# 512-column products with v, row-by-row reads of the second merge branch, and a later place in the queue for the pairs of the last product, in an encoder layer on Trainium2

## The chip, the cores and the metric

The kernel is one program on one core of a Trainium2 chip. The metric is device time in microseconds (us). The kernel before took 1592.64 us in the median of three runs (1591.06 to 1593.86). Rates and waits below come from one profiled execution of it, read with the hardware profiler.

## The reference

The reference is one layer of an encoder with three branches, for two sequences of 512 rows and 1024 columns each. Cut to what matters here:

```python
h = rmsnorm(x) @ w_in
u, q, k, v, xq, g = split(h)                      # g: three gates of 1024 columns
y_s5 = s5_branch(u)                               # state-space scan, both directions
w = softmax(q0 @ k0.T) - lam * softmax(q1 @ k1.T) # 4 heads, two maps each
y_diff = rmsnorm(w @ v) * (1 - lambda_init)       # 4 heads of 128 columns
y_x = cross_attention(xq, mem)
merged = sum(sigmoid(g[n]) * (branch[n] @ w_up[n]) for n in range(3))
x = x + merged @ w_out
gate, up = split(rmsnorm(x) @ w_ffn_in)           # 2816 columns each
x = x + (silu(gate) * up) @ w_ffn_out
out = rmsnorm(x)
```

All data is float32, and the result has to have nearly float32 precision.

## The kernel before, in words

**Precision.** TensorE multiplies in a reduced float32 format (fp32r). Each operand is therefore split into a high and a low part: ScalarE (ACT) rounds the source to the high part and VectorE (DVE) subtracts it for the low part (`split`, lines 134 to 138). One product is then three matmuls: high by high, high by low, low by high. A matmul has 128x128 weights and streams 512 columns, or 256 in the products with v. Every matmul and every transpose is issued through one helper (lines 66 and 69), so in the profile they all have one of these two lines, and they are told apart by the tiles in their names. Nearly all of the order of TensorE's work from the attention on is the order in the code (`InOrder`).

**Attention.** For each of 4 heads and 2 sequences there are 4 steps of 128 query rows (`qt` 0 to 3). A step i of the loop near line 915 does: scores for two steps at once (every other step), ten further matmuls or so from a queue of other work (`fill`), then `turn(i)`, then `outputs(i - 1)` after every second step, then more filling. `turn` transposes the 128x512 weights of the softmax on TensorE into a bank named `tr` (seen as `bktr`), and splits them into `pH` and `pL`; a pair of these tiles holds two steps, 256 columns, and there are four buffers, two pairs. `outputs` multiplies one such pair by v: 12 matmuls of 256 columns (tiles `bkoo<-pH,vh` and so on). It runs twice per head and sequence, in two halves of one bank, and ScalarE copies the bank to `osb` after the second (line 892). `squares` and `normed` (line 911) then normalise `osb` and write it to DRAM (`bD`).

**Merge.** Other work in that queue is `merges`: for each of 8 column tiles m, first branch 0, then branch 2, later branch 1. `merge_units` reads a gate row `gl` (1024 columns, 512 KB) into the ring `ld`, which has four slots, and multiplies the products by it on VectorE (line 796). The branches themselves are read as rows `yt` into the same four slots and split into `yh`, `yl` (line 773 the read, lines 137 and 138 the split). Branch 2's four rows are read and split together ahead of tile m = 2 of branch 0.

**Feed-forward.** 22 iterations, 19 us each, make seven products of a Strassen-like scheme (`SEVEN`) for each 128 rows of hidden units. GpSimd (POOL) makes sums of the weights (`ws`, lines 1040 to 1043) and multiplies `up` (line 1182). From iteration 4 on, a `half_piece` per iteration also prepares raw weights of the last product: sums on POOL (lines 454 to 457), splits, and a write to DRAM (`wD`). It is held behind two instructions of the iteration, the tanh and the last sum. The activations `ac` are written to DRAM tiles `aD[0..21]`.

**Last product.** `VISITS` lists 12 visits v of an output tile, 36 pieces in all, each a pair p of hidden tiles. A piece is 21 matmuls: seven products, three matmuls each. It needs three things: its prepared weights `w` (pieces 0 to 15 come whole from `wD`, two reads of 384 and 512 KB, lines 1255 and 1253; pieces 16 to 27 half; pieces 28 to 35 are prepared on the spot from raw weights), the pair's activations, and room. A pair is two reads of 512 KB (`fa` and `fb`, lines 1139 and 1140), four sums on VectorE and POOL (lines 989 to 992) and four splits into `th` and `tl`. Pairs 3 to 8 are brought in by `pair_in` at set places of the loop. After visits, VectorE and POOL add the seven banks into `y` (lines 1120 and 1308).

**Who issues reads.** Nearly all DMAs are issued by SyncE (SP), which takes its list in order and waits where a buffer is not free yet. The list is built by a scheduler; `queued()` means that what is issued inside it stands behind the last weight read issued so far (`last_w`). `tc.issue_after(x)` holds instructions behind x in their engines' lists.

## Time and profile before

| | |
|---|---|
| median of three runs | 1592.64 us (1591.06 to 1593.86) |
| the profiled execution | 1595.11 us |
| its span in the trace | 1593.3 us, so 1.8 us lie around the span |
| TensorE busy | 99% of the span, 7838 matmuls and transposes |
| VectorE, ScalarE, GpSimd busy | 73%, 40%, 33% |
| mean granted TensorE clock | 0.996 |
| DMA | 237.84 MB, 149 GB/s in the mean |

The granted clock is given as a share of full speed. Matmuls are pipelined: a matmul of 512 columns is shown 0.39 us long, but the next one starts about 0.23 us after it. How long a stretch of matmuls takes is therefore read from starts, and a stall is a start that comes later than that. "SPq" rows are DMA issues; how long a transfer takes from its issue to its landing is a separate figure of the trace.

### The profile page before, as it was taken

The numbers are of one execution on the slowest core, as the hardware profiler recorded it, in microseconds if no ns is written. First come the engines' busy times: TensorE is split into PE (matmuls) and PEld (weight loads), VectorE is DVE, ScalarE is ACT, GpSimd is POOL, SyncE is SP. The second block draws the span as 40 slices with busy tenths as digits, with TensorE's granted clock in tenths as the row PEclk, the third lists the DMA queues.
The fourth block names the chain that finished last, engine by engine and source line by source line (L and its number), as shares of the span: only waits on it lengthen the run. The fifth ranks groups of instructions, "written<-read, shape, count | busy, mean of one in ns | idle before, by whom it ended". The sixth has DMA issues, their size and how long they took to land.

```text
span 1593.3 us, 21527 instructions
## 1 busy us (share of the span) xinstructions
PE 1577.1 (99%) x7838; PEld 1317.1 (83%) x7838; DVE 1162.6 (73%) x1858; ACT 631.0 (40%) x1114; POOL 532.9 (33%) x434
## 2 busy tenths in 40 slices
PE   9999999999999999999999999999999999999997
PEld 7888888888898789878888888888888888788787
DVE  7978995077773776865545578888888878978864
ACT  6644223275652465563223343233332333223323
POOL 0010000001333320300443355766676543444663
PEclk9999999999999999999999999999999999999998
DMA  9554623576762121154543522333333323985312
GB/s 363 178 167 127 205 93 124 177 265 209 255 225 102 52 89 41 47 162 149 192 145 119 146 85 94 108 104 120 119 129 124 111 93 116 331 320 190 125 60 106
DMA packets 104890, 237.84 MB, mean 149 GB/s; under 512 B 13520, under 2 KB 45008, under 8 KB 104784
## 3 DMA queue, kind: packets, MB, share of 16 engines
q1 hardware_dynamic: 104784, 236.47, 44.0%
q8 instruction: 61, 1.00, 0.3%
q14 instruction: 45, 0.37, 0.1%
HBM read 165.16 MB, written 71.27 MB: 148 GB/s over the span
## 4 chain that ended last, share of the span: by engine, by line
PE 90%; DVE 3%; POOL 3%; DMA 2%; issue 1%; SPq 0%; ACT 0%; POOLq 0%; DVEq 0%; ACTq 0%
PE bkmm L66 78%; PE bktr L66 4%; PE bkoo L66 2%; PE bktr L69 2%; PE bksc L66 1%; PE bktr L1673 1%; DMA w<-wD 1%; DVE wl L135 1%; PE bktr L1642 1%; DMA aD<-ac 1%; PE bktr L1734 0%; PE bktr L1733 0%; PE bktr L1732 0%; PE bktr L1609 0%; DMA mt<-in_memT 0%
## 5 line engine op out<-in xcount | busy, mean ns | idle before, releaser
L66 PE MATMUL bkmm<-xh,wh 128*128 128x512 f32 x640 | 254.4, 398 | 0.0
L66 PE MATMUL bkmm<-xh,wl 128*128 128x512 f32 x640 | 250.5, 392 | 0.0
L66 PE MATMUL bkmm<-xl,wh 128*128 128x512 f32 x640 | 250.1, 391 | 0.0
L66 PE MATMUL bkmm<-th,wl 128*128 128x512 f32 (+1 forms) x621 | 240.9, 388 | 0.6 <-DVE wl L135 0.6
L66 PE MATMUL bkmm<-tl,wh 128*128 128x512 f32 (+1 forms) x621 | 241.1, 388 | 0.0
L66 PE MATMUL bkmm<-th,wh 128*128 128x512 f32 (+1 forms) x621 | 240.7, 388 | 0.0
L134 ACT CAST wh<-wf 128x1024 fp32r<-128x1024 f32 (+1 forms) x133 | 117.4, 883 | 245.2 <-PE bkmm L66 178.5
L135 DVE TENSOR_TENSOR wl<-wf,wh 128x1024 fp32r<-128x1024 f32 (+1 forms) x133 | 149.9, 1127 | 61.3 <-ACT wh L134 56.9
L66 PE MATMUL bkmm<-th,w 128*128 128x512 f32 x432 | 142.1, 395 | 3.4 <-DMA w<-wD 2.7
L66 PEld LDWEIGHTS bkmm<-xh,wh 128*128 128x128 f32 x640 | 120.3, 188 | 26.2 <-issue 3.4
L66 PEld LDWEIGHTS bkmm<-xh,wl 128*128 128x128 f32 x640 | 120.2, 188 | 26.1 <-issue 0.4
L66 PEld LDWEIGHTS bkmm<-xl,wh 128*128 128x128 f32 x640 | 120.4, 188 | 22.2
L66 PEld LDWEIGHTS bkmm<-th,wl 128*128 128x128 f32 x621 | 116.5, 188 | 25.0 <-DVE wl L135 1.1
L66 PEld LDWEIGHTS bkmm<-tl,wh 128*128 128x128 f32 x621 | 116.6, 188 | 24.0
L66 PEld LDWEIGHTS bkmm<-th,wh 128*128 128x128 f32 x621 | 116.6, 188 | 23.8
L454 POOL TENSOR_TENSOR raw<-raw 128x128 f32<-128x128 f32 x28 | 15.9, 572 | 312.4 <-DVE nb L545 230.2
L1182 POOL TENSOR_TENSOR up<-up,acc 128x512 f32<-128x512 f32 x44 | 82.4, 1891 | 80.1 <-DVE up L1120 76.4
L66 PEld LDWEIGHTS bkmm<-th,w 128*128 128x128 f32 x432 | 81.7, 189 | 24.3 <-DMA w<-wD 3.4
L800 POOL TENSOR_TENSOR mg<-mg,gl 128x1024 f32<-128x1024 f32 x16 | 43.8, 2739 | 138.3 <-DVE gl L796 133.7
L66 PE MATMUL bkmm<-tl,w 128*128 128x512 f32 x216 | 84.7, 392 | 0.0
L66 PE MATMUL bkmm<-yh,wh 128*128 128x512 f32 x192 | 76.1, 396 | 0.0
L1181 ACT ACTIVATE ac<-gf 128x512 f32<-128x512 f32 x44 | 27.8, 633 | 119.5 <-DVE gf L1180 61.0
(661 smaller groups left out, 3563.6 us busy)
## 6 DMA issues: line engine op xcount, KB each, us to landing
wf<-in_w_in SPq DMA_DIRECT2D x40, 512.0 KB, 4.0
wD<-hl SPq DMA_DIRECT2D x28, 512.0 KB, 2.9
w<-wD SPq DMA_DIRECT2D x28, 512.0 KB, 4.7
gD<-gt SPq DMA_DIRECT2D x24, 512.0 KB, 3.0
gl<-gD SPq DMA_DIRECT2D x24, 512.0 KB, 3.4
wf<-in_w_fg SPq DMA_DIRECT2D x22, 512.0 KB, 3.7
wf<-in_w_fu SPq DMA_DIRECT2D x22, 512.0 KB, 3.7
aD<-ac SPq DMA_DIRECT2D x22, 512.0 KB, 3.0
```

Source lines behind the costliest of these rows:

```text
L66: return self.put(self.eng.matmul(*args, **kw))
L69: return self.put(self.eng.transpose(*args, **kw))
L134: h = S.copy(hi, src)
L135: l_ = V.tensor_tensor(out=lo, in0=src, in1=hi.bitcast(F32), op=ALU.subtract)
L454: PO.tensor_tensor(out=a22, in0=a21, in1=a22, op=ALU.add)
L800: PO.tensor_tensor(out=mg[m], in0=mg[m], in1=gt, op=ALU.add)
L1181: last_t = S.activation(out=ac[:, cs], in_=gf, func=AF.Tanh, scale=0.5)
L1182: PO.tensor_tensor(out=up, in0=up, in1=accs[s], op=ALU.mult)
L1642: PE.matmul(kp[64 * hf : 64 * hf + 48, g * 144 : (g + 1) * 144], l48[:, ri, 4 * g4 + 2 * hf + g, :], o_[:, 4 * g4 + 2 * hf + g, :], start= ...
L1673: PE.matmul(ps[:, g * P : (g + 1) * P], w_[:, gg * P : (gg + 1) * P], u_[:, 8 * o + gg, :], start=True, stop=True)
```

## The change

Four edits:

1. `outputs` runs once per head and sequence: 12 matmuls of 512 columns on one pair `pH`, `pL` of 512 columns (two buffers in place of four, the same memory). It stands ahead of `turn` in a step, and ScalarE copies its bank right behind it.
2. Branch 2's rows are no longer read and split together ahead of tile 2. Row 0 is read after tile 3 and split after tile 4, row 1 after tile 4 and split after tile 5, rows 2 and 3 after tile 5 and split after tile 6.
3. `half_piece` stands behind a third instruction too, the last multiplication of `up` on POOL.
4. `pair_in` of pairs 3 to 8 and the write of `aD[21]` are put behind the weight reads issued so far (`queued()`).

```diff
-    open_tags(phase, v2=2, qk=12, pT=4)
+    open_tags(phase, v2=2, qk=12, pT=2)
...
         for m in range(KD):
-            if m == 2:
-                b2 = merge_in(2)
             yield from merge_units(0, b0, m, first=True)
+            for t in {4: (0,), 5: (1,), 6: (2, 3)}.get(m, ()):
+                merge_split(b2, 2, t, "y", b2_in[t])
+            for t in {3: (0,), 4: (1,), 5: (2, 3)}.get(m, ()):
+                b2_in[t] = merge_load(2, t)
...
     def turn(i):
         h, s, qt = steps[i]
-        if qt % 2 == 0:
-            pT[h, s, qt // 2] = tuple(slot("pT", [P, 4, 2 * P], F32R, n_) for n_ in ("pH", "pL"))
+        if qt == 0:
+            pT[h, s] = tuple(slot("pT", [P, 4, L], F32R, n_) for n_ in ("pH", "pL"))
...
     def outputs(i):
...
-        if qt == 1:
-            osb[h, s] = bank("oo")
-        od = osb[h, s][:, qt // 2 * 2 * P : (qt // 2 + 1) * 2 * P]
+        od = bank("oo")
...
-        if qt == 3:
-            o_ = rp.tile([P, L], F32, tag="nsq", name="osb", bufs=2)
-            S.copy(o_, osb[h, s])
-            osb[h, s] = o_
+        osb[h, s] = rp.tile([P, L], F32, tag="nsq", name="osb", bufs=2)
+        S.copy(osb[h, s], od)
...
         fill(10 if i < n - 1 else 16)
+        if 0 < i <= n and steps[i - 1][2] == 3:
+            outputs(i - 1)
         if 0 <= i < n:
             turn(i)
-        if 0 < i <= n and steps[i - 1][2] % 2:
-            outputs(i - 1)
...
-            PO.tensor_tensor(out=up, in0=up, in1=accs[s], op=ALU.mult)
+            last_u = PO.tensor_tensor(out=up, in0=up, in1=accs[s], op=ALU.mult)
...
         if 4 <= i < KFF - 3:
-            half_piece((last_t, last_sum))
+            half_piece((last_t, last_sum, last_u))
...
             if v == 3 and p == 0:
-                with tc.issue_after(last_sum.ins):
+                with queued(), tc.issue_after(last_sum.ins):
                     pair_in()
...
         if v == 2:
-            nc.sync.dma_start(aD[KFF - 1], ac)
+            with queued():
+                nc.sync.dma_start(aD[KFF - 1], ac)
...
         if v in (3, 4, 6, 7):
-            with tc.issue_after(last_sum.ins):
+            with queued(), tc.issue_after(last_sum.ins):
                 pair_in()
```

What this does to the order on SP is seen where pair 3 is read, in the last product. In the list of before, from pair 3 (`fa<-aD_9207`) on (the number behind `wD_` and the next one name the pair and the piece's tile; `128x768` and `128x1024` are the two reads of one piece, and `wD_2_3008` belongs to piece 7):

```order
L1139 DMA fa<-aD_9207 128x1024
L1140 DMA fb<-aD_9208 128x1024
L1318 DMA aD_9222<-ac 128x1024
L1139 DMA fa<-aD_9209 128x1024
L1140 DMA fb<-aD_9210 128x1024
L1255 DMA w_12843<-wD_2_3008 128x768
L1253 DMA w_12844<-wD_2_3008 128x1024
L1255 DMA w_12868<-wD_0_3009 128x768
```

The list of the change from the same place on (its lines are numbered 8 lower; pair 3 is `aD_9095`, pair 4 `aD_9097` and `aD_9098`):

```order
L1131 DMA fa<-aD_9095 128x1024
L1132 DMA fb<-aD_9096 128x1024
L1247 DMA w_12731<-wD_2_3008 128x768
L1245 DMA w_12732<-wD_2_3008 128x1024
L1247 DMA w_12756<-wD_0_3009 128x768
L1285 DMA y_12467<-x1D 128x1024
L1245 DMA w_12757<-wD_0_3009 128x1024
L1247 DMA w_12783<-wD_1_3010 128x768
L1311 DMA aD_9110<-ac 128x1024
L1245 DMA w_12784<-wD_1_3010 128x1024
L1247 DMA w_12836<-wD_2_3011 128x768
L1131 DMA fa<-aD_9097 128x1024
```

The write of `aD[21]` and both reads of pair 4 stood ahead of piece 7's weights; the write now stands between piece 9's two reads, and pair 4 between those of piece 10. Further on, pair 5 moves into the reads of piece 13, pair 6 behind those of piece 16, pair 7 behind piece 22, pair 8 behind piece 25.

On VectorE the second edit is seen ahead of the line that normalises `osb`, the third such line in the merge of branch 0. Before (`yl` are the splits of branch 2's rows):

```order
L135 TENSOR_TENSOR pL<-bktr,pH 128x4x128
L138 SCALAR_TENSOR_TENSOR yl_7432<-yt,yh_7431 128x1024
L138 SCALAR_TENSOR_TENSOR yl_7438<-yt,yh_7437 128x1024
L796 SCALAR_TENSOR_TENSOR mg_7328<-gl,bkmm 128x512
L138 SCALAR_TENSOR_TENSOR yl_7444<-yt,yh_7443 128x1024
L911 SCALAR_TENSOR_TENSOR osb<-osb,g_3470,bktr 128x512
L543 TENSOR_REDUCE nb<-bktr 128x1
```

And in the change:

```order
L135 TENSOR_TENSOR pL<-bktr,pH 128x4x128
L790 SCALAR_TENSOR_TENSOR mg_7229<-gl,bkmm 128x512
L903 SCALAR_TENSOR_TENSOR osb<-osb,g_3470,bktr 128x512
L138 SCALAR_TENSOR_TENSOR yl_7541<-yt,yh_7540 128x1024
L543 TENSOR_REDUCE nb<-bktr 128x1
```

The normalisation stands ahead of all four splits, and one split follows it at once.

On POOL the third edit is seen in iteration 4 of the feed-forward, where the first raw weights are summed (`raw`, four tiles of four sums). Before:

```order
L1040 TENSOR_TENSOR ws<-wf 128x512
L1043 TENSOR_TENSOR ws<-wf 128x512
L454 TENSOR_TENSOR raw<-raw 128x128
L1041 TENSOR_TENSOR ws<-ws,wf 128x512
L454 TENSOR_TENSOR raw<-raw 128x128 x3
L455 TENSOR_TENSOR raw<-raw 128x128
L1042 TENSOR_TENSOR ws<-wf,ws 128x512
L455 TENSOR_TENSOR raw<-raw 128x128 x3
L456 TENSOR_TENSOR raw<-raw 128x128 x4
L457 TENSOR_TENSOR raw<-raw 128x128 x4
L1182 TENSOR_TENSOR up<-up,acc 128x512 x2
```

And in the change:

```order
L1174 TENSOR_TENSOR up<-up,acc 128x512 x2
L1032 TENSOR_TENSOR ws<-wf 128x512
L1035 TENSOR_TENSOR ws<-wf 128x512
L1033 TENSOR_TENSOR ws<-ws,wf 128x512
L1034 TENSOR_TENSOR ws<-wf,ws 128x512
L1174 TENSOR_TENSOR up<-up,acc 128x512
L454 TENSOR_TENSOR raw<-raw 128x128
L455 TENSOR_TENSOR raw<-raw 128x128
L1174 TENSOR_TENSOR up<-up,acc 128x512
L456 TENSOR_TENSOR raw<-raw 128x128
L457 TENSOR_TENSOR raw<-raw 128x128
```

Both multiplications of `up` of that iteration stand ahead of the sums, which are spread: one tile per iteration, between the two multiplications of the next.

More of the change, by code (lines that the diff above doesn't have):

```diff
@@ L779, in merge_split @@
         b[0][t], b[1][t] = h_, l_
-    def merge_in(n, tags="yyyy"):
-        b = [None] * 4, [None] * 4
-        for t in range(4):
-            merge_split(b, n, t, tags[t], merge_load(n, t))
-        return b
     def merge_units(n, b, m, first=False, last=False):
@@ L806, in encoder @@
     mes, zes = ExitStack(), ExitStack()
-    b0, b1 = (([None] * 4, [None] * 4) for _ in range(2))
+    b0, b1, b2 = (([None] * 4, [None] * 4) for _ in range(3))
+    b2_in = {}
     b1_in = []
@@ L871, in turn @@
             PE.transpose(tr[:, j * P : (j + 1) * P], e0[:, j * P : (j + 1) * P], ident)
-        ps = slice(qt % 2 * P, qt % 2 * P + P)
-        split(*(p_[:, :, ps] for p_ in pT[h, s, qt // 2]), tr.rearrange("p (j q) -> p j q", j=4))
+        split(*(p_[:, :, qt * P : (qt + 1) * P] for p_ in pT[h, s]), tr.rearrange("p (j q) -> p j q", j=4))
     def outputs(i):
-        h, s, qt = steps[i]
-        if h == 2 and s == qt - 1 == 0:
+        h, s, _ = steps[i]
+        if h == 2 and s == 0:
             finish(v1_)
@@ L881, in outputs @@
         vs = slice((h % 2) * P, (h % 2) * P + P)
-        pH, pL = pT.pop((h, s, qt // 2))
-        if qt == 1:
-            osb[h, s] = bank("oo")
-        od = osb[h, s][:, qt // 2 * 2 * P : (qt // 2 + 1) * 2 * P]
+        pH, pL = pT.pop((h, s))
+        od = bank("oo")
         for j in range(4):
@@ L1150, in all7 @@
         return w
-    nxt_w, last_t = res0, None
+    nxt_w, last_t, last_u = res0, None, None
     for i in range(KFF):
@@ L1177, in activate @@
         def activate(s, gf, up):
-            nonlocal last_t
+            nonlocal last_t, last_u
             cs = slice(s * L, (s + 1) * L)
```

## The prediction, as it was put on record

> **What bounds the kernel now.** I read the totals first, then the chain of waits, then what TensorE (PE) waited for, then each of those places in the timeline.
>
> ```profile
> PE 1577.1 (99%) x7838; PEld 1317.1 (83%) x7838; DVE 1162.6 (73%) x1858; ACT 631.0 (40%) x1114; POOL 532.9 (33%) x434
> ...
> PE 90%; DVE 3%; POOL 3%; DMA 2%; issue 1%; SPq 0%; ACT 0%; POOLq 0%; DVEq 0%; ACTq 0%
> ...
> PE bkmm L66 <- DMA w<-wD: 2.7, 3, 2.2
> PE bktr L69 <- DVE osb L911: 0.9, 1, 0.9
> PE bkmm L66 <- DVE wl L135: 0.6, 1, 0.6
> PE bkmm L66 <- ACT w L137: 0.3, 1, 0.3
> ```
>
> PE is busy for 99% of the span and holds 90% of the chain. The last four rows are all of its waits between 100 and 1580 us: 4.5 us in six waits. So the change can win in two ways only: fewer PE cycles, or one of these few waits. They name three of the four places that it touches.
>
> The largest is in the last product, at pieces 6 and 7:
>
> ```profile
> 1376.34 3.41 PE bkmm L66 x15
> ...
> 1383.29 10.77 DMA w<-wD
> ...
> 1385.69 0.39 PE L66 MATMUL bkmm<-th,w 128*128 128x512 f32 x1
> ...
> 1390.23 0.39 PE L66 MATMUL bktr<-th,w 128*128 128x512 f32 x1
> 1392.80 0.50 PE L66 MATMUL bkmm<-th,w 128*128 128x512 f32 x1 [2.19 <-DMA w<-wD]
> ...
> 1394.10 0.79 PE L66 MATMUL bkmm<-th,w 128*128 128x512 f32 x1 [0.33 <-DMA w<-wD]
> ...
> 1395.12 1.05 PE L66 MATMUL bkmm<-th,w 128*128 128x512 f32 x2
> ...
> 1399.87 0.39 PE L66 MATMUL bkmm<-th,w 128*128 128x512 f32 x1
> ```
>
> The first row, of the chain, gives the pace: 15 matmuls in 3.41 us, 0.227 us each. Piece 6 starts at 1385.69 and piece 8 at 1399.87: 42 matmuls in 14.18 us, where 42 x 0.227 makes 9.55. The two pieces lose 4.6 us: a wait of about 2.3 us for piece 7's first read, about half a microsecond for its second (the chain's row: issued 1383.29, 10.77 us to landing), and then a slow stretch: from 1394.10 to 1399.87 there are 18 matmuls in 5.77 us, where 4.09 would do (the two of 1395.12 are shown at 1.05 us).
>
> **The last product, term 1.** Why piece 7's weights are late is seen in SP's list and in the rate:
>
> ```profile
> 1380.57 0.43 SPq L1140 DMA_DIRECT2D fb<-aD  x1
> 1381.09 0.53 SPq L1318 DMA_DIRECT2D aD<-ac  x1
> ...
> DMA to landing us min/median/max: 7.5/7.5/7.5
> ...
> GB/s 393 355 388 344 104 85 261 76 315 389 408 382 295 213 273 388 426 410 426 421 400 421 421 410 415 431 408 426 432 404 431 415 410 423 411 427 410 429 396 87
> ```
>
> The rate row cuts 1375 to 1405 us into 40 slices: from 1386 on it stays at 396 to 432 GB/s. The queue is full, and 512 KB take 1.25 us at 420 GB/s. Pair 3's second read (issued 1380.57, landed 7.5 us later) comes in at 1388.1. Between it and piece 7's reads stand a 512 KB write (1381.09) and, by SP's list above, pair 4's two reads: 1.5 MB, 3.75 us. The change takes all three out. Then piece 7's 384 KB land at 1388.1 + 0.9 = 1389.0 and its 512 KB at 1390.3. The first is needed at 1390.46, the second three matmuls later, at 1391.1 (1394.10 is the fourth matmul of the piece). Both are in time, by 1.4 and 0.8 us. **Gain 4.6 us.**
>
> What is late next? Pieces 8 to 13 ask 896 KB in 4.77 us each, 192 GB/s; with the write, pairs 4 and 5 and four `y` rows between 1390 and 1419 that is some 360 GB/s of 410, so the backlog shrinks. By hand, at 1.25 us for 512 KB, the reads of pieces 8 to 11 land 1 to 3 us ahead of need. Pair 4 lands near 1402 and is first needed by piece 14, which starts near 1424 now. Pair 5 lands near 1417 and is needed near 1438. This cover is gone only if the rate falls well below 400 GB/s.
>
> The clock gate of the Trainium skill (TensorE: Matmul & The Clock Gate, Part 1) lowers the clock after an idle window of about 3.4 us and restores it after about 3.4 us of work. By the first half, an idle stretch of 2.3 us would cost no slow stretch, and this term would be an estimated 2.9 us; the rows from 1394.10 on show the slow stretch, so I keep 4.6.
>
> **Products with v, term 2.**
>
> ```profile
> L66 PE MATMUL bkoo<-pH,vh x64: 277/283/368, 540.6 to 750.3; 128*128 128x256 f32 x64
> ...
> 540.83 1.43 PE bkoo L66 x12
> 542.26 2.75 PE bkmm L66 x12
> ```
>
> 64 of each of the three kinds make 192 matmuls of 256 columns, 16 groups of 12. A group takes 1.43 us, 0.119 each, while 12 matmuls of 512 columns take 2.75. Two groups become one: 2.86 against 2.75, 0.11 us, eight times. **Gain 0.9 us.** The bounds: nothing, if the 512-column products pay the wait for a new bank, and twice that, 1.8 us, if half of the starts are freed from another cost. I take the row.
>
> The same page (Back-to-back issue gap) gives N / 2.4 + 2.5 ns for one matmul alone: an estimated 109 ns for 256 columns and 216 for 512, so eight pairs of groups would win 0.25 us; the rows' 119 ns says that a short matmul costs more here.
>
> With one pair `pH`, `pL` the next step's ACT cast must wait until the 12 products have read the old one. It costs nothing on PE: the cast's own transposes stand behind these 12 products in the new order, so the pair is free when they end. The copy to `osb` stands ahead of that cast and delays it by its 0.59 us, while PE has ten matmuls of filling, 2.3 us.
>
> **The merge, term 3.**
>
> ```profile
> 711.55 1.06 ACT L137 ACTIVATE yh<-yt 128x1024 fp32r<-128x1024 f32 x1 [0.23 <-DMA yt<-bD]
> ...
> 713.10 1.22 DVE L138 SCALAR_TENSOR_TENSOR yl<-yt,yh 128x1024 fp32r<-128x1024 f32 x1
> 714.23 0.74 DVE L911 SCALAR_TENSOR_TENSOR osb<-osb,g,bktr 128x512 f32<-128x512 f32 x1
> ...
> 713.70 0.40 PE L66 MATMUL bkmm<-yh,wl 128*128 128x512 f32 x1
> 715.03 0.66 PE L69 MATMUL bktr<-ident,e 128*128 128x128 f32 x4 [0.93 <-DVE osb L911]
> ...
> DMA to landing us min/median/max: 3.2/3.5/4.2
> ...
> 719.00 0.68 DVE L796 SCALAR_TENSOR_TENSOR mg<-gl,bkmm 128x512 f32<-128x512 f32 x1
> 721.89 0.59 ACT L134 CAST pH<-bktr 128x512 fp32r<-128x512 f32 x1 [2.49 <-PE bktr L69]
> 729.05 0.60 PE L69 MATMUL bktr<-ident,e 128*128 128x128 f32 x4
> ```
>
> The transposes at 715.03 wait for a bank that `osb` on DVE frees. DVE took it up at 714.23 because splits of branch 2's rows stood ahead, of which the last (713.10) could only start behind ACT's cast of 711.55, which had waited for the row's read. In the new list `osb` stands ahead of all of them. The stall is 715.03 - 713.70 - 0.23 = **1.1 us, gained**.
>
> The price: rows 1 to 3 now reach ACT between casts and exponentials. Row 1's slot in the ring is free after tile 1's second sum on DVE, at 719.7 here (the row of 719.00); such a read takes 3.5 us to land (the row above is of `gl` reads of the same size from 719 to 733 us), so it lands near 723. ACT stands before it in order, then casts for 1.06 us, so the `pH` cast of 721.89 comes near 724.7. PE's next transposes are those of 729.05, so I count nothing; if it needed it at once, the cost would be 2.8 us here and about as much at row 3, where the reads come in the same way. The bounds are 0 and 5.6; I take 0.3.
>
> **Feed-forward, term 4.**
>
> ```profile
> 1014.07 2.52 POOL L1182 TENSOR_TENSOR up<-up,acc 128x512 f32<-128x512 f32 x2
> ...
> 1021.44 0.39 PE L66 MATMUL bkmm<-tl,wh 128*128 128x512 f32 x1
> 1022.39 0.50 PE L66 MATMUL bkmm<-th,wl 128*128 128x512 f32 x1 [0.56 <-DVE wl L135]
> ```
>
> `up` stood behind sixteen raw sums until 1014.07; DVE waited for it and split weights late. PE lost 1022.39 - 1021.44 - 0.23 = **0.7 us, gained**, as `up` is now ahead of the sums. In the other iterations two small sums of about 0.5 us now stand between the two `up`, so DVE waits 1 to 2 us longer there. PE waits for DVE in no other iteration (the waits above), so that slack covers it. Uncovered, 14 iterations at 1 us would be 14 us; nothing in the waits suggests it.
>
> **The end of the last product.**
>
> ```profile
> 1460.00:1480.00 20.00, 20.00 (x90) 16.58 (x89) 19.80 (x25) 6.28 (x9) 12.45 (x9) 1.00 0.62 193
> ...
> 1471.46 0.33 SPq L1253 DMA_DIRECT2D w<-wD x1
> ...
> 1478.46 1.18 DVE L989 TENSOR_TENSOR ts<-fa 128x512 f32<-128x512 f32 x1
> ...
> 1488.62 0.55 DVE L138 SCALAR_TENSOR_TENSOR w<-acc,w 128x384 fp32r<-128x384 f32 x1
> ...
> 1490.47 4.09 PE bkmm L66 x18
> 1494.56 0.56 DVE w L138
> ...
> 1522.41 3.23 PE bkmm L66 x13
> ```
>
> From 1494.56 to 1522.41 the chain runs over DVE, POOL and ACT: raw weights of pieces 28 to 33. Term 1 counts only if this work comes 4.6 us earlier too. It should: in 1460 to 1480 DVE works 19.80 of 20 us (the third number after the stretch), but it begins there with sums of PE's banks, and the chain enters the preparation from PE. Pair 8 is now read behind piece 25's weights, where before stands 1471.46. Two reads of 512 KB behind one that takes 4.9 us land at 1477.6 to 1478.9 in that clock; DVE takes them up at 1478.46, behind visit 7's sums. So it is just in time; I allow 0.2 us, and with term 3's 0.3, 0.5 in all.
>
> **The sum.** 4.6 + 0.9 + 1.1 + 0.7 - 0.5 = 6.8 us. The profiled execution took 1595.11 us (a span of 1593.3 and 1.8 around it), so its like would take 1588.3. It lies 2.5 us above the median, so I predict 1592.64 - 6.8 = **1585.8 us**.
>
> **Rivals.**
>
> (a) The gain is given back at the end. If DVE and POOL set the pace from 1460 on by themselves, PE arrives early at pieces 27 to 33 and waits there: all of term 1 is lost, 1590.4. For it: 19.80 of 20 and a chain off PE. Against it: DVE's start with PE's sums. Chance 0.16.
>
> (b) The queue stays full and weights are still late, at pieces 7 to 11. At 350 GB/s in place of 415, 512 KB take 1.5 us, piece 7's second read comes at 1390.8 and pieces 9 to 11 use up their margins: 1 to 2 us return, 1587.3. Chance 0.12.
>
> (c) ACT stands before rows 1 and 3 and PE waits: 2.8 to 5.6 us return, about 4.2 us in place of the 0.3, 1589.7. Chance 0.10.
>
> (d) Slower: pair 8 comes too late. From DVE's 1478.46 to 1488.62 the work is back to back, and everything behind it, the splits and raw sums of pieces 26 to 33, moves with it: each microsecond past 1478.5 is one of PE. If the pair's reads go out two pieces later than I read (9.5 us) or wait for the sums of an older pair, PE loses that, and pair 5, with about 1.2 us in hand, loses some 3 more: 1585.8 + 12, 1598. It passes the time of before from 6.8 us of delay. Against it: its two waits, POOL's sums of pair 6 and a landed read, are long over by 1471. Chance 0.08.
>
> (e) The change does not do what it says, as the new 512-column products gain nothing and `osb` is late for another reason: 1587.8. Chance 0.06.
>
> **How the numbers follow.** The forecast has the other 0.48. A difference under 0.2% (3.2 us, about what a measurement of this kernel can tell) is no change. Faster by more, below 1589.45: the forecast, (b), (e) and half of (c), 0.71. Within: most of (a) and half of (c), 0.19. Slower: (d) and a little of (a), 0.10. The range goes from 1582.0, where term 2 is double, the 0.5 is not paid and the late waits go, to 1594.3, where (a) and (c) fall together; (d) is left out. The late waits are 2.5 us: pieces 27 to 33 run from 1490.47 to 1522.41 + 3.23 + 0.68 = 1526.32, 35.85 us, where seven pieces make 33.4.
>
> **What would show it.** Right: no wait of PE for `w<-wD` near 1390 and pieces 6 and 7 of 4.77 us each, with no slow matmuls behind; transposes near 711 without a wait for `osb`; 96 matmuls of 512 columns in `bkoo`; no wait for `wl` in iteration 5; pieces 27 to 33 in about 35.9 us. Wrong: waits for `w` from ACT or DVE near pieces 26 to 33 that sum to over 3 us, a wait for `tl` or `th` of pairs 5 to 8, or one for `bktr` on ACT's `pH` between 720 and 740.

## The result, and the profile after

The changed kernel takes 1610.7 us (median of six runs, 1606.11 to 1612.68) beside 1593.25 us of the kernel before on the same chip (six runs, 1588.79 to 1594.49). The ratio is 1.0112, 95% interval 1.0094 to 1.013: it is **slower by 17.5 us**, where 6.8 us less were forecast. The profiled execution took 1610.45 us, near its median; the one of before that the prediction was built on, 1595.11 us, lies 2.5 us above the median of the three runs known then (1592.64).

The totals and the chain of the page:

```profile
PE 1580.4 (98%) x7742; PEld 1309.9 (81%) x7742; DVE 1175.5 (73%) x1858; ACT 627.0 (39%) x1114; POOL 539.1 (34%) x434
...
PE 75%; DVE 7%; POOL 6%; DMA 5%; issue 5%; ACT 1%; SPq 0%; POOLq 0%; ACTq 0%; DVEq 0%
```

PE is still busy for 98%, but its share of the chain fell from 90% to 75%: for part of the time another loop now sets the pace. PE's waits between 100 and 1580 us show where (in total, how often, the longest):

```profile
PE bkmm L66 <- DVE wl L135: 13.3, 16, 1.8
PE bkmm L66 <- DVE mg L790: 1.3, 1, 1.3
PE bkmm L66 <- ACT p L1118: 1.2, 1, 1.2
PE bktr L69 <- DVE rs L199: 1.2, 1, 1.2
PE bkmm L66 <- DVE nsq L1112: 0.2, 1, 0.2
```

The wait for `w<-wD` (2.7 us before) and the one for `osb` are gone, as forecast. In their place stand 16 waits for `wl`, the split weights of the feed-forward; before there was one. Four of the five rows can be seen in PE's timeline, where a matmul that waits for nothing starts 0.23 us after the one ahead:

```profile
715.90 0.39 PE L66 MATMUL bkmm<-yh,wl 128*128 128x512 f32 x1
717.60 0.50 PE L66 MATMUL bkmm<-yh,wh 128*128 128x512 f32 x1 [1.31 <-DVE mg L790]
...
736.25 0.39 PE L66 MATMUL bkmm<-yh,wl 128*128 128x512 f32 x1
737.80 0.65 PE L69 MATMUL bktr<-ident,rs 128*128 128x128 f32 x4 [1.16 <-DVE rs L199]
...
1162.77 0.39 PE L66 MATMUL bkmm<-tl,wh 128*128 128x512 f32 x1
1163.89 0.50 PE L66 MATMUL bkmm<-th,wl 128*128 128x512 f32 x1 [0.73 <-DVE wl L135]
...
1404.78 0.39 PE L66 MATMUL bkmm<-th,w 128*128 128x512 f32 x1
...
1414.30 0.39 PE L66 MATMUL bkmm<-th,w 128*128 128x512 f32 x1
...
1509.27 0.39 PE L66 MATMUL bktr<-th,w 128*128 128x512 f32 x1
1510.84 0.50 PE L66 MATMUL bkmm<-th,w 128*128 128x512 f32 x1 [1.17 <-ACT p L1118]
```

In order: two new waits in the merge (1.47 and 1.32 us over the pace), one of the 16 in the feed-forward, pieces 6 and 7 of the last product (from 1404.78 to 1414.30, 9.52 us, no loss), and a new wait ahead of piece 28.

Where the time went, by the start of the first matmul of a stage in the two profiled executions (us):

| stage | before | after | difference |
|---|---|---|---|
| start of the merge's branch 0 | 699.33 | 698.37 | -0.96 |
| feed-forward, iteration 0 | 934.09 | 934.52 | +0.43 |
| iteration 5 | 1032.95 | 1032.53 | -0.43 |
| iteration 8 | 1090.07 | 1090.64 | +0.57 |
| iteration 12 | 1166.23 | 1174.45 | +8.22 |
| last product | 1356.65 | 1375.99 | +19.34 |
| end of the trace | 1593.33 | 1608.68 | +15.35 |

The attention gains, the merge loses 1.4, iteration 4 gains 0.86 (the 0.7 of term 4), iterations 7 to 18 lose 19.8, and the last product gives 4.0 back (most of it the luck of that execution before: in a second profile of the kernel before the last product takes 3.3 us less than here, see edit 4 below). One iteration lasts 20.9 us there (8.22 - 0.57 is 7.65 in four iterations, 1.9 each, on top of 19.04).

### Why an iteration takes 20.9 us

POOL's timeline in iteration 10, first of the kernel before, then of the changed one:

```profile
1142.04 0.46 POOL L454 TENSOR_TENSOR raw<-raw 128x128 f32<-128x128 f32 x1 [3.62 <-DMA raw<-in_w_fo]
...
1144.94 3.92 POOL L1182 TENSOR_TENSOR up<-up,acc 128x512 f32<-128x512 f32 x2 [0.47 <-DVE up L1120]
1151.54 1.65 POOL L1040 TENSOR_TENSOR ws<-wf 128x512 f32<-128x512 f32 x1 [2.69 <-DMA wf<-in_w_fu]
...
1156.68 1.62 POOL L1042 TENSOR_TENSOR ws<-wf,ws 128x512 f32<-128x512 f32 x1
```

```profile
1156.29 2.19 POOL L1174 TENSOR_TENSOR up<-up,acc 128x512 f32<-128x512 f32 x1 [7.10 <-DVE up L1112]
1158.44 0.91 POOL L454 TENSOR_TENSOR raw<-raw 128x128 f32<-128x128 f32 x1
1159.43 0.46 POOL L455 TENSOR_TENSOR raw<-raw 128x128 f32<-128x128 f32 x1
1159.85 1.29 POOL L1174 TENSOR_TENSOR up<-up,acc 128x512 f32<-128x512 f32 x1
...
1162.64 2.34 POOL L1032 TENSOR_TENSOR ws<-wf 128x512 f32<-128x512 f32 x1 [0.22 <-DMA wf<-in_w_fu]
```

Before, the raw sums ran in a stretch where POOL waited anyway for DVE's `up`. The third condition names the multiplication that the code issues last, of the second sequence; its operand is ready first, and POOL runs it first. So the sums land between the two, 1.4 us in front of one that DVE waits for. DVE's rows from there on, before and after:

```profile
1148.88 0.69 DVE L1184 TENSOR_TENSOR ac<-ac,up 128x512 f32<-128x512 f32 x1 [1.19 <-POOL up L1182]
...
1150.21 0.69 DVE L1180 TENSOR_TENSOR gf<-gf,acc 128x512 f32<-128x512 f32 x1
1150.82 1.22 DVE L135 TENSOR_TENSOR wl<-ws,wh 128x1024 fp32r<-128x1024 f32 x1
...
1157.07 0.68 DVE L1120 TENSOR_TENSOR u<-bkmm,p 128x512 f32<-128x512 f32 x1
```

```profile
1161.17 0.93 DVE L1176 TENSOR_TENSOR ac<-ac,up 128x512 f32<-128x512 f32 x1 [2.14 <-POOL up L1174]
...
1162.63 1.21 DVE L135 TENSOR_TENSOR wl<-ws,wh 128x1024 fp32r<-128x1024 f32 x1
1163.76 1.77 DVE L1172 TENSOR_TENSOR gf<-gf,acc 128x512 f32<-128x512 f32 x1
...
1166.23 1.01 DVE L1175 SCALAR_TENSOR_TENSOR ac<-ac,gf 128x512 f32<-128x512 f32 x1 [0.70 <-ACT ac L1173]
```

DVE waits 2.14 us in place of 1.19, at the lower end of what the prediction had ("1 to 2 us longer"). The wait matters because `ac` is one tile: it cannot be written again before the write of the last iteration's `ac` to DRAM has landed. The tanh that writes it first shows this on ACT, at the two ends of one turn, before (first fence) and after (second):

```profile
1141.70 0.63 ACT L1181 ACTIVATE ac<-gf 128x512 f32<-128x512 f32 x1 [4.32 <-DMA aD<-ac]
...
1160.61 0.63 ACT L1181 ACTIVATE ac<-gf 128x512 f32<-128x512 f32 x1 [4.19 <-DMA aD<-ac]
```

```profile
1153.06 0.63 ACT L1173 ACTIVATE ac<-gf 128x512 f32<-128x512 f32 x1 [6.30 <-DMA aD<-ac]
...
1174.10 0.63 ACT L1173 ACTIVATE ac<-gf 128x512 f32<-128x512 f32 x1 [6.44 <-DMA aD<-ac]
```

From tanh to tanh is a closed loop: tanh, ACT's casts behind it, DVE's splits and `up`, POOL's `up`, DVE's `ac`, the write, the next tanh. This turn took 18.91 us before, beside PE's 19.04, and takes 21.04 us after. Turns are not all alike, as the write lands 2.6 to 4.8 us after its issue: the nine turns that begin in iterations 7 to 15 take 18.1 to 20.2 us before, 19.0 in the mean, and 20.3 to 21.6 after, 20.9 in the mean. So the loop had no time to spare in the mean. What looked like slack was a lead: in iteration 9 of the kernel before, DVE's split of two of the weight sums (S3 and S4) ended at 1113.42 and the matmul that needs it started at 1117.73, 4.3 us later. In the changed kernel that lead is 3.8 us in iteration 5, 1.7 in iteration 6 and gone in iteration 7; a loop that is 2 us too long uses it up in two or three iterations, and each later one costs its full excess.

### The profile page after: what moved, and what is told of

Same layout as the page of the kernel before. It is cut to its first block, busy times and chain, and to the rows that moved or that the text cites. A ratio compares the mean times of both kernels' runs of the same rounds, so it can differ in the third digit from the quotient of the medians.

```text
span 1608.7 us, 21318 instructions
## 1 busy us (share of the span) xinstructions
PE 1580.4 (98%) x7742; PEld 1309.9 (81%) x7742; DVE 1175.5 (73%) x1858; ACT 627.0 (39%) x1114; POOL 539.1 (34%) x434
## 4 chain that ended last, share of the span: by engine, by line
PE 75%; DVE 7%; POOL 6%; DMA 5%; issue 5%; ACT 1%; SPq 0%; POOLq 0%; ACTq 0%; DVEq 0%
PE bkmm L66 63%; PE bktr L66 3%; POOL up L1174 2%; DMA aD<-ac 2%; PE bkoo L66 2%; PE bktr L69 2%; DVE wl L135 2%; PE bksc L66 1%; DMA wf<-in_w_fu 1%; DMA yt<-bD 1%; DVE gf L1172 1%; PE bktr L1666 1%; DVE ac L1175 1%; DVE ac L1176 1%; DVE hl L138 1%
## 5 line engine op out<-in xcount | busy, mean ns | idle before, releaser
L66 PE MATMUL bkmm<-th,wl 128*128 128x512 f32 (+1 forms) x621 | 243.3, 392 | 13.5 <-DVE wl L135 13.3
L135 DVE TENSOR_TENSOR wl<-wf,wh 128x1024 fp32r<-128x1024 f32 (+1 forms) x133 | 153.8, 1156 | 61.8 <-ACT wh L134 56.9
L1174 POOL TENSOR_TENSOR up<-up,acc 128x512 f32<-128x512 f32 x44 | 78.7, 1797 | 148.2 <-DVE up L1112 144.5
```

The lines of the kernel that those rows point to most:

```text
L66: return self.put(self.eng.matmul(*args, **kw))
L135: l_ = V.tensor_tensor(out=lo, in0=src, in1=hi.bitcast(F32), op=ALU.subtract)
L1174: last_u = PO.tensor_tensor(out=up, in0=up, in1=accs[s], op=ALU.mult)
```

## The experiments

The theory after the two traces, theory 1: edit 3 costs the time, by sums that stand inside the loop through `ac`; the other edits are worth a few microseconds at most. Rivals: the loss lies in the other edits or in their meeting; or DVE's own work, not the loop, sets the new pace. Each run is set against runs of the kernel before on the same chip.

| run | us | before | ratio, 95% interval |
|---|---|---|---|
| edit 3 alone | 1607.46 | 1593.08 | 1.0089 (1.0074 to 1.0104) |
| all but edit 3 | 1592.26 | 1593.08 | 0.9996 (0.9987 to 1.0005) |
| all, `ac` in two tiles | 1595.96 | 1593.08 | 1.0021 (1.0013 to 1.003) |
| edit 4 alone | 1592.09 | 1593.08 | 0.9993 (0.9984 to 1.0003) |
| edit 2 alone | 1596.36 | 1594.3 | 1.0011 (1.0002 to 1.002) |
| edit 1 alone | 1593.38 | 1594.3 | 0.9997 (0.9988 to 1.0005) |
| all, sums behind both `up` | 1592.56 | 1594.3 | 0.9989 (0.998 to 0.9998) |
| edits 1, 4 and 3 behind both `up` | 1590.99 | 1594.57 | 0.9977 (0.9969 to 0.9986) |
| the same, pair 8 not queued | 1590.09 | 1594.57 | 0.9974 (0.9963 to 0.9984) |
| all, DVE's order as before | 1614.63 | 1593.38 | 1.0125 (1.0102 to 1.0148) |

**Edit 3 alone**, in the kernel before:

```diff
-            PO.tensor_tensor(out=up, in0=up, in1=accs[s], op=ALU.mult)
+            last_u = PO.tensor_tensor(out=up, in0=up, in1=accs[s], op=ALU.mult)
...
-            half_piece((last_t, last_sum))
+            half_piece((last_t, last_sum, last_u))
```

> The kernel before with the third edit alone (the prepared sums of the feed-forward also behind the last multiplication of up on POOL). Theory 1 (a loop): in iterations 4 to 18 the tanh of one iteration must wait until the one tile ac of the iteration before has been written to DRAM; the sums now stand between the two multiplications of up inside that loop and stretch it from 19.0 to some 20.9 us, so TensorE loses about 19 us between the seventh and the nineteenth iteration, whatever the other edits do: 1593 + 19 = 1612 us, a ratio near 1.012, with about 18 waits for wl on VectorE. Rival (it needs the other edits): the same lists of the engines without the later reads of pairs and the 512-column products lose nothing, 1592 to 1593 us.

It is slower by 14 us, and its profile has the same waits:

```profile
PE bkmm L66 <- DVE wl L135: 8.8, 14, 0.8
```

In its trace iterations 9 to 17 lose 13.5 us, after a gain of 0.86 in iteration 4. Edit 3 holds most of the loss. It starts to lose two iterations later than the changed kernel, and loses 13.5 in place of 19.8 us. The difference lies in the turns of the loop: the three that begin in iterations 4 to 6 are 4.7 us longer together in the changed kernel, the nine behind them 0.2 us each. Why they are longer, no run shows.

**All but edit 3**, the changed kernel with one line put back:

```diff
-            half_piece((last_t, last_sum, last_u))
+            half_piece((last_t, last_sum))
```

> The changed kernel without its third edit. If the third edit is the whole loss, the feed-forward is as before (one wait of 0.7 us for wl in iteration 5, 19.04 us per iteration) and the rest stays as in the changed kernel: -0.9 us for the products with v, +1.7 for the merge (waits of 1.5 and 1.3 us in place of one of 1.1), -3.5 for the last product: about 1590.5 us, ratio 0.998 (0.996 to 1.000). Rival: if the feed-forward was lengthened by another edit too, waits for wl remain and the time stays above 1600 us.

The time is that of the kernel before within the measurement (0.13% less to 0.05% more), and the feed-forward loses nothing. So the other three edits together win nothing that this measurement can tell, where some 6 us were forecast for them.

**The loop cut.** The changed kernel with `ac` as two tiles of 512 columns, each written to DRAM by itself, so that the tanh of one half no longer waits for the write of both:

```diff
-        ac = ap2.tile([P, NT], F32, tag="ac", name="ac")
+        ac = [ap2.tile([P, L], F32, tag=f"ac{s}", name=f"ac{s}") for s in range(NS)]
...
-        nc.sync.dma_start(aD[i], ac)
+        for s in range(NS):
+            nc.sync.dma_start(aD[i][:, s * L : (s + 1) * L], ac[s])
...
```

> The changed kernel with the tile ac made of two tiles of 512 columns, each written to DRAM by itself, so that the tanh of the next iteration's first half waits only for the write of the first half, which is asked for some 8 us earlier; the engines' lists stay as they are. Theory 1 (the loop through ac): the loop is cut, the waits for wl between iterations 7 and 19 go, and the time falls by about 18 to 20 us to about 1591. Rival (throughput or order: the raw sums between the two multiplications and the swapped places on VectorE cost their time by themselves, in every iteration): the waits stay, 1608 to 1612 us.

PE's waits for `wl`, and ACT's tanh at the two ends of one turn:

```profile
PE bkmm L66 <- DVE wl L135: 3.7, 4, 1.6
```

```profile
1184.49 0.63 ACT L1173 ACTIVATE ac<-gf 128x512 f32<-128x512 f32 x1 [4.94 <-DVE gf L1172]
...
1204.41 0.63 ACT L1173 ACTIVATE ac<-gf 128x512 f32<-128x512 f32 x1 [4.94 <-DVE gf L1172]
```

Sixteen waits become four, and the feed-forward loses 4.9 us in place of 19.8. The sums still stand between the two `up`; with the loop cut, three quarters of the loss is gone, so the loop through `ac` carried it. The tanh now waits for DVE, and a turn takes 19.92 us: DVE's list, with its waits for POOL, is the next loop, 0.9 us over PE's pace; it loses less than 0.9 us in each iteration because it uses up a lead first.

**Edit 4 alone**, the three places of `queued()` in the kernel before:

```diff
-                with tc.issue_after(last_sum.ins):
+                with queued(), tc.issue_after(last_sum.ins):
...
+            with queued():
+                nc.sync.dma_start(aD[KFF - 1], ac)
...
-            with tc.issue_after(last_sum.ins):
+            with queued(), tc.issue_after(last_sum.ins):
```

> The kernel before with the fourth edit alone (reads of pairs 3 to 8 and the last write of activations behind the weight reads). If the prediction's first term holds by itself: no wait for piece 7's weights, pieces 6 and 7 of 4.76 us each, 4.6 us won there; the later reads of pair 8 give some 1.2 us back at pieces 27 and 28 as in the changed kernel: 1593.2 - 3.5 = 1589.7 us, ratio 0.998. Rival: if the gain in the changed kernel came only because its slower feed-forward left the queue emptier, the wait stays and the time is that of before.

Pieces 6 and 7 take 4.76 us each: the wait for `w<-wD` is away. But the time falls by 1.0 us only (the interval: 2.5 less to 0.5 more). Two things take the rest. Pieces 27 and 28 last 5.83 and 6.05 us, where they take 4.76 and 5.09 with edit 2 alone (piece 30 gives 0.9 us of that back). And the wait that was removed is not always as long as in the first profile, as a second profile of the kernel before shows:

> The kernel before, profiled once more. The later reads of pairs won 3.3 us in the trace but only 1.0 us in the median of the timed runs. Theory: the wait for piece 7's weights in the kernel before depends on how full the queue is and differs from one execution to the next, and the profiled one, 2.5 us above its median, had a long one: here pieces 6 and 7 lose 1 to 4 us, less than 4.6. Rival: they lose 4.6 us again, and the gain is lost elsewhere in the timed runs.

```profile
PE bkmm L66 <- DMA w<-wD: 0.6, 2, 0.3
```

Pieces 6 and 7 lose 1.2 us there, in place of 4.6, and this execution took 1592.3 us. In the runs that kept the reads as they were, these two pieces lose 4.5 (edit 3 alone), 2.9 (edit 2 alone) and 0.9 us (edit 1 alone). Two things differ. The wait for piece 7's first read is 2.35 us in the first profile, 2.6 and 2.2 with edits 3 and 2 alone, and under 0.5 in the other two. And the slow stretch behind it is a lower granted clock (the number ahead of the last two of this row):

```profile
1394.00:1397.00 3.00, 2.90 (x7) 2.32 (x8) 0.69 (x1) 0.45 (x1) 1.28 (x1) 0.51 1.03 423
```

The clock fell so in the first profile and with edit 3 alone, for 3.4 us each, which costs 1.7 us; with edit 2 alone it stayed at 1.00. In the traces the last product takes 232.7 to 234.0 us in the seven kernels with the whole of edit 4, and 232.9 to 237.9 in the five without it, so the edit takes away the long ones.

**Edit 2 alone**, the row-by-row reads in the kernel before:

```diff
-            if m == 2:
-                b2 = merge_in(2)
...
+            for t in {4: (0,), 5: (1,), 6: (2, 3)}.get(m, ()):
+                merge_split(b2, 2, t, "y", b2_in[t])
+            for t in {3: (0,), 4: (1,), 5: (2, 3)}.get(m, ()):
+                b2_in[t] = merge_load(2, t)
```

> The kernel before with the second edit alone (rows of branch 2 read one by one behind tiles 3 to 5). Theory 1: each row's read waits for a slot of the ring of four that a sum of the tile before frees, lands 3.4 to 4.8 us later, and ACT and VectorE stand before its cast and split in order; TensorE pays about 1.5 us for a bank near 716 and about 1.3 us for one near 737, and wins the 1.1 us near 714: +1.5 to +2 us in the trace at the end of the merge, 1593 to 1596 us, ratio 1.000 to 1.002. Rival (the prediction's own term, and the waits of the changed kernel come from the products with v that now stand ahead of the turn): -1.1 us and no new wait, 1592.

It is slower by 0.11% (0.02 to 0.2), some 1.8 us. Its waits:

```profile
PE bkmm L66 <- DVE mg L790: 1.3, 1, 1.3
PE bktr L69 <- DVE osb L908: 0.8, 1, 0.8
```

The wait for `osb` does not go: in the seven traces with the rows read together it is 0.6 to 2.3 us, so 0.8 is no gain. With edit 2 alone `osb` still stands behind the first split on DVE, which waits for ACT's cast of row 0:

```profile
712.52 1.23 DVE L138 SCALAR_TENSOR_TENSOR yl<-yt,yh 128x1024 fp32r<-128x1024 f32 x1 [1.77 <-ACT yh L137]
713.67 0.74 DVE L908 SCALAR_TENSOR_TENSOR osb<-osb,g,bktr 128x512 f32<-128x512 f32 x1
```

It stands ahead of all splits, and the wait is gone, only in the five traces with edits 1 and 2 together. The new wait, for `mg`, comes at 733.58, behind the split of row 2. From the start of the merge to the feed-forward PE takes 236.1 to 236.9 us in the six traces with edit 2 and 234.4 to 235.9 in the seven without.

In the changed kernel the waits come at rows 0 and 3. The mechanism is seen in ACT's timeline there:

```profile
710.52 1.06 ACT L137 ACTIVATE yh<-yt 128x1024 fp32r<-128x1024 f32 x1 [4.53 <-DMA yt<-bD]
...
713.48 0.69 ACT L548 ACTIVATE e<-bktr,nb 128x512 f32<-128x512 f32 x1 [0.59 <-DVE nb L543]
...
734.95 1.06 ACT L137 ACTIVATE yh<-yt 128x1024 fp32r<-128x1024 f32 x1 [1.74 <-DMA yt<-bD]
736.03 1.28 ACT L198 ACT_TABLE_LOAD   x1
```

ACT stands 4.53 us before row 0 and 1.74 us before row 3. Behind the first stand exponentials and the cast `pH`, and on DVE the split `pL` of it with `mg` right behind; behind the other a table load and `rs`. PE's waits at 717.60 and 737.80 are these two.

**Edit 1 alone**, the 512-column products in the kernel before:

```diff
-        if qt % 2 == 0:
-            pT[h, s, qt // 2] = tuple(slot("pT", [P, 4, 2 * P], F32R, n_) for n_ in ("pH", "pL"))
+        if qt == 0:
+            pT[h, s] = tuple(slot("pT", [P, 4, L], F32R, n_) for n_ in ("pH", "pL"))
```

(and the other lines of that edit)

> The kernel before with the first edit alone (products with v once per head and sequence). By the prediction's term: 96 matmuls in place of 192, -0.9 us at the end of the attention, no new wait, 1592.2 us, ratio 0.9994. Rival (the one pair of buffers, or the copy ahead of the cast, costs a wait per product): 0 to +1 us, with waits for bktr or for pH between 540 and 760 us.

The medians differ by 0.9 us, which is within the measurement (0.12% less to 0.05% more). In the trace the start of the merge comes 0.55 us earlier. All traces agree: from the first scores to the start of the merge, with six of the eight products between them, PE takes 320.6 us in the five without edit 1 and 320.0 in the eight with it.

**The sums behind both multiplications**, the changed kernel with edit 3 put right:

```diff
-            last_u = PO.tensor_tensor(out=up, in0=up, in1=accs[s], op=ALU.mult)
+            last_us[s] = PO.tensor_tensor(out=up, in0=up, in1=accs[s], op=ALU.mult)
...
-            half_piece((last_t, last_sum, last_u))
+            half_piece((last_t, last_sum, last_us[0], last_us[1]))
```

> The changed kernel, with the prepared sums held behind both multiplications of up instead of only the one called last (which POOL does first). Theory 1a: cutting the write of ac won 14.9 of 19.8 us of the trace, and what is left is VectorE's own list: its work of 17 us per iteration and a wait of 2.1 us for the second multiplication, which stands behind two raw sums on POOL, make 19.9 us, more than TensorE's 19.04. With the sums behind both, that wait falls to the 1.2 us of before and both loops are short enough: no waits for wl after iteration 7, the time of the changed kernel without its third edit or up to 1 us less, 1591 to 1592.5 us. Rival (the sums cost their time wherever they stand behind a multiplication, as the sums ws for the next weights come 2 us later on POOL): waits for wl remain, 1598 to 1608 us.

POOL and DVE in iteration 10:

```profile
1145.40 3.90 POOL L1174 TENSOR_TENSOR up<-up,acc 128x512 f32<-128x512 f32 x2 [5.40 <-DVE up L1112]
1149.26 0.46 POOL L454 TENSOR_TENSOR raw<-raw 128x128 f32<-128x128 f32 x1
```

```profile
1149.33 0.94 DVE L1176 TENSOR_TENSOR ac<-ac,up 128x512 f32<-128x512 f32 x1 [1.18 <-POOL up L1174]
```

DVE waits 1.18 us, as before, and from iteration 5 to the last product the kernel loses 0.4 us. The gain of 0.86 in iteration 4 stays. But the loop is not short enough: its turns take 19.5 us in the mean of iterations 7 to 15, more than PE's 19.04, as the sums now run beside DVE's `gf` and split (0.77 and 1.48 us in most of these turns, 0.69 and 1.22 before). The lead carries it: that of S3 and S4 falls from 4.8 us in iteration 5 to 0.05 in iteration 15. A longer feed-forward would lose some 0.4 us in each further iteration, an estimate from 19.5 less 19.04. One more instruction named in the condition moves the ratio from 1.0112 to 0.9989, some 19 us: the place of the sums is the cause, not the condition as such.

**The edits that win, together.** Edits 1 and 4 and the mended edit 3, without edit 2; and the same with pair 8 alone left out of `queued()`, as in the kernel before:

```diff
-            with queued(), tc.issue_after(last_sum.ins):
+            with queued() if v < 7 else ExitStack(), tc.issue_after(last_sum.ins):
```

> The kernel before with edit 1 (512-column products), edit 3 with the prepared sums held behind both multiplications of `up`, and edit 4 (`queued()`), without edit 2 (branch 2's rows stay read and split together ahead of tile 2). Theory 1 (edit 3 as made costs the time, by sums that stand between the two multiplications; all else is worth a few us at most and its gains do not take each other's place): edit 1 gives 0.6 to 0.9 us, iteration 5's wait 0.9 us less some 0.4, edit 4 1 to 3 us less 1.2 for pair 8: 2 to 4 us in all, 1589 to 1591 beside 1593, ratio about 0.998, and in the feed-forward no more than one wait for `wl`. Rival (edit 4 and edit 1 lose against each other at the end of the last product, pieces 27 to 33): within 1 us of the kernel before, ratio 0.9995 to 1.0005, with over 5 us of waits from piece 26 on. Second rival (the gain of edit 4 is there only where the execution has the long wait of pieces 6 and 7): the trace shows pieces 6 and 7 at 4.8 us each, and the median time moves by under 1.5 us.

> The kernel of the run before (edits 1, 3 with both multiplications first, and 4) with pair 8 alone not queued behind the weight reads. If pair 8's late reads cost the 1.2 us seen at pieces 27 and 28 in each kernel with edit 4, these two pieces take 5.6 us or so in place of 6.0 to 6.2 each, and the time is up to 1.2 us below that of the run before (ratio to the kernel before lower by about 0.0005 to 0.0008). If those waits come from the preparation on VectorE and GpSimd whatever the time at which pair 8 lands, both pieces stay as they are and the time is the same within 0.5 us.

Both beat the kernel before, by 0.23% (0.14 to 0.31) and 0.26% (0.16 to 0.37). The first wins 3.6 us, within the 2 to 4 of theory 1, with edit 2 left out, which costs 1.8 by itself. The second is the fastest kernel of this study, 1590.09 beside 1594.57 us. Pieces 27 and 28 take 6.05 and 6.04 us in the first, 4.76 and 5.19 in the second, whose read of pair 8 is issued at 1455.15 in place of 1466.36: pair 8's late read makes those waits. Of the 2.1 us won there, piece 30 gives 0.8 back (5.74 in place of 4.90), and the times differ by 0.9 us, less than their intervals.

**DVE's order.** After the change the scheduler puts the split `wl<-ws` ahead of `gf<-gf,acc` on DVE, seen in the rows of 1162.63 and 1163.76. The turn shown above grew by 2.13 us and the wait for `up` by 0.95 only; the rest I put down to that order. This run puts it back (`after` is the last `gf<-gf,acc`):

```diff
...
+                h = S.copy(wh[:, :n], src)
+                with tc.issue_after(after.ins):
+                    last_s = (h, V.tensor_tensor(out=wl[:, :n], in0=src, in1=wh[:, :n].bitcast(F32), op=ALU.subtract))
...
-        sp(aps, s34, "s", "S3", "S4")
+        sp(aps, s34, "s", "S3", "S4", after=last_g if i > 4 else None)
...
```

> The changed kernel with one thing more: from iteration 5 on VectorE's split of S3 and S4 (`wl<-ws`) is held behind the multiplication `gf<-gf,acc` of the second sequence, as the kernel before has them; GpSimd's list, its sums between the two `up` among them, is as in the changed kernel, and ScalarE's list has the copy of `p` behind the tanh again, as before. In the changed kernel one turn of the loop through `ac` grew from 18.9 to 21.0 us: 0.95 by VectorE's longer wait for `up` (2.14 in place of 1.19), the rest by what stands behind it, where `gf<-gf,acc` comes after the split, runs beside GpSimd's `ws` (1.77 in place of 0.69 us) and lets VectorE wait 0.70 us for the tanh. Theory 1 (both parts count, the sums' time and the order that the scheduler then chose): a turn takes some 19.9 us, 0.9 over TensorE's 19.04; with a lead of 4.3 us to use up first, 12 iterations lose 5 to 8 us in place of 19.8, some 1597 to 1600 us, ratio 1.002 to 1.005. Rival (the sums between the two `up` alone cost it and the order does nothing): the loss stays at 18 to 20 us, ratio 1.010 to 1.013. Second rival (the order alone costs it): the loss in the feed-forward is under 1 us, ratio 0.999 to 1.0005.

The rival held: nothing is won, the feed-forward loses 21.5 us, and a turn takes 21.1 us in the mean of iterations 7 to 15. DVE's rows say why:

```profile
1164.02 0.69 DVE L1177 TENSOR_TENSOR gf<-gf,acc 128x512 f32<-128x512 f32 x1
1164.63 2.31 DVE L1029 TENSOR_TENSOR wl<-ws,wh 128x1024 fp32r<-128x1024 f32 x1
```

Now `gf` takes 0.69 us again here, and in six of iterations 5 to 15 (some 1.7 in the other five), but the split takes 2.31 in place of 1.21, and some 2.3 in all of them. Whatever stands there runs beside POOL's `ws` sums, which begin 1.5 us after the second `up` ends in the changed kernel and 2.7 us after it before. So that part of my account, the order as a cause of its own, falls. That the other 1.1 us of a turn come from one more DVE instruction running beside POOL is read from these rows; a run that takes it away alone was not made.

## Why the prediction was wrong

**The failing step is the cover in term 4**: "PE waits for DVE in no other iteration (the waits above), so that slack covers it." The mechanism ahead of it was right (sums between the two `up`, which took 0.91 and 0.46 us for the 0.5 each of the text, and DVE later by 1 us), and the gain at 1021 us came (0.86 for 0.7). What failed is reading "no wait" as slack. The loop took 19.0 us a turn in the mean, all of PE's 19.04, and the 4 us or so that weights were early are spent once, not anew in each iteration. "Uncovered, 14 iterations at 1 us would be 14 us; nothing in the waits suggests it": the runs showed 19.8, as a turn grew by 1.9 us in the mean, and the rows that suggested it were not waits of PE but of ACT, whose tanh waited 1.7 to 5.2 us for the write of `ac` in each of iterations 5 to 17. It had no rival and no chance, though its price stood in the text.

**Term 1 (4.6 us)**: the mechanism was right, the size off. The wait left, pieces 6 and 7 took 4.76 us. But the price was taken from one execution, in which they lost 4.6; four others lose 0.9, 1.2, 2.9 and 4.5. Of the 4.6, 1.7 us were the lower granted clock behind the wait, which came in two of the five; the 2.9 us that the text named as its other reading are what the execution with nearly the same wait and a full clock lost. So the size was that execution's luck. The text noted that this execution lay 2.5 us above the median, and took the full wait off the median all the same. (The rate row reads 388 in the slice from 1386.25 and 87 in the last, outside the 396 to 432 of the text; nothing rests on it.) By itself the edit is worth 1.0 us (2.5 less to 0.5 more).

**The end of the last product (0.2 us)**: rival (d)'s place and mechanism, at a tenth of its price. Pair 8 is late by too little to lose 12 us; pieces 27 and 28 lose 2.6 us together in the changed kernel, where 0.5 was lost before, and the run with pair 8 early takes that away.

**Term 2 (0.9 us)**: right, 0.1 us for each product: 0.6 us for the six ahead of the merge, in all traces alike. The 512-column products stand in the trace as forecast:

```profile
L66 PE MATMUL bkoo<-pH,vh x32: 389/389/396, 552.2 to 750.4; 128*128 128x512 f32 x32
```

**Term 3 (1.1 us gained for 0.3)**: the wait for `osb` went in the changed kernel, though edit 2 alone did not take it away, and its size too was read from one execution (0.6 to 2.3 us in seven). The price was 2.8 us (1.47 and 1.32), inside the bounds of 0 to 5.6. The wrong part was the choice of 0.3: the row of 729.05 was taken for PE's next need, but the exponentials and the table load behind ACT's wait feed DVE's sums that PE needs first, and row 0 was the first to be waited for, not row 1. The working of the price has a slip: 719.7, 3.5 and 1.06 make 724.3, not 724.7, and so 2.4 us, not 2.8.

**The rivals**: (b) and (e) did not come; (c) came, at rows 0 and 3 for its 1 and 3, with 2.8 us for its 2.8 to 5.6. (a) did not come as told: pieces 27 to 33 take 37.0 us in place of 35.9, and that is pair 8's share. The slower side was given to one mechanism of small size, while the 14 us in the text were left out of the chances.

## What to carry to other kernels

No wait on the engine that bounds a kernel does not say that its feeders have time to spare: find the loop that closes through a single buffer (here `ac` and its write to DRAM), take its turn from one instruction to its next, in the mean of several, and compare that with the pace. An early result is a lead that is spent once; a cost that comes in each iteration needs room in each turn. Where two like instructions are issued in one order and run in another, hold new work behind both, and take the size of a wait from several executions before it is counted as a gain.

## What the runs showed of the hardware

DVE and POOL slow each other where both work on SBUF data. A DVE operation of two 128x512 inputs takes 0.69 us alone and 1.77 beside POOL's `ws` sums (the rows of 1150.21 and 1163.76); a split of 1024 columns 1.21 and 2.31. In these rows the engine that begins second pays: the split that begins at 1162.63, just ahead of POOL's sum of 1162.64, takes 1.21 us and the sum 2.34. The median sum in the kernel before takes 1.74 us, the shortest 1.29 (minimum, median and maximum in ns):

```profile
L1043 POOL TENSOR_TENSOR ws<-wf x16: 1291/1736/1747, 1038.9 to 1322.9; 128x512 f32<-128x512 f32 x16
```

The Trainium skill (SBUF — State Buffer, SBUF: two separate sides) says that the two engines share one pair of ports as an exclusive lock, held for a whole instruction; the rows agree as far as they go: the engine that comes second takes nearly the sum of both times (0.69 and 1.29 make 1.98, the rows have 1.77 and 1.74), and a DVE operation with only one of its inputs there, the other in one of PE's banks, keeps its 0.68 us beside such a sum (`u<-bkmm,p` at 1157.07, the sum from 1156.68 to 1158.30).

Not expected was how much the loss by a wait for DMA differs from one execution of a kernel to the next: 4.6 and 1.2 us at pieces 6 and 7 in two profiles of the same kernel, in a stretch where the queue is full.

TensorE's granted clock can fall behind a short wait. Between 100 and 1580 us of all these traces it fell five times, to 0.50 for 3.4 us: behind waits of 2.35 us (the kernel before, with a wait of 0.5 us close behind), 2.6 (edit 3 alone), and 2.65 to 2.9 (three times with DVE's order as before). It did not fall behind waits of 2.2 (edit 2 alone), 2.40 (DVE's order) and 2.44 us (pair 8 not queued). So a wait of this length can cost 1.7 us more than itself, or not.
